# Layer-1 MLP: the second product with tokens on the partitions, seven eighths of it by Strassen's seven block products

## Chip, core and metric

The kernel runs on one core of a Trainium2 chip. The metric is the device time of one execution in microseconds (us). The engines are TensorE (PE; PEld is its weight load), VectorE (DVE), ScalarE (ACT), GpSimd (POOL) and SyncE (SP, which issues most of the DMAs).

## What is computed

The program is a two-layer trunk over 512 latent and 256 context tokens of width 1024. Layer 0 mixes by an mLSTM, layer 1 by windowed attention, and each layer ends in a squared-ReLU MLP of inner width 4096. The change touches only the MLP of layer 1, on the 512 latent tokens, and what follows it:

```
h   = h + gate_msa * attention(...)
u   = rms_norm(h, norm_ffn) * (1 + scale) + shift      # 512 x 1024
hid = square(relu(u @ w1))                             # 512 x 4096
h   = h + gate * (hid @ w2)                            # 512 x 1024
out = rms_norm(h, final_norm)                          # 512 x 1024
```

## The kernel before, in words

Every fp32 product runs in three passes: each operand is split into a rounded part and a rest (`split`, L927 on ACT makes the high part, L928 on DVE the low part), and `mm3` (L96 to L98) multiplies high by high, high by low and low by high into one PSUM bank. Weights come in units of 128x1024 (512 KB): `unit` starts a DMA from SP into one of three `raw` buffers and splits it into one of four pairs `whi`, `wlo` (`nraw` and `nsplit` in `open_ring`).

In layer 1 the hidden stream lies transposed: features on the partitions, 512 tokens along the free axis, in eight tiles `hL`. `ffn` loops over four chunks of 1024 hidden features. In a chunk, the first `dense` makes eight tiles of `hid` from eight units of `w1`, 24 matmuls of 512 columns each; `evac1` does relu on ACT (L901), the square on POOL (L902), and the split into `hH`, `hL_` on ACT and DVE (L904, L905). The second `dense` multiplies the chunk by eight units of `w2`, 24 matmuls each, and `evac2` adds each result, times its gate, to `hL` on DVE (L912). The first three units of the first chunk and the last two of the last are done in two halves of 256 tokens, A and B, so that the norm ahead (`norm_group`) and the norm behind overlap with matmuls. In the last chunk `norm_add` (L302, L306) sums squares, `norm_rc` (L319 to L324) and `norm_bc` (L332) make 1/rms by matmuls with ones, a power on POOL and a transpose back, and `final` (L1646, L1650) scales each `hL` tile and writes it out from the SP and ACT queues.

The order on each engine is fixed ahead of the run by a scheduler that works from the program's dependencies; an engine then takes its rows strictly in that order. Waits come from semaphores, and a tile's buffer is reused when its last reader is done.

## Time and profile before

| what | value |
|---|---|
| time, median of 3 runs | 1590.76 us (1590.04 to 1591.33) |
| the profiled execution: time, span | 1593.31 us, 1591.5 us |
| mean granted TensorE clock | 0.988 |
| busy share of the span: PE, PEld, DVE, ACT, POOL | 97%, 87%, 64%, 42%, 25% |

The span is cut in stretches to see which engine has idle time where; the chain that ended last and the groups of instructions say what one operation takes. PE's durations overlap (a matmul starts before the one ahead has ended), so the time of one matmul is read from the distance of two starts.

### The profile page before, as it was taken

The page shows a single profiled execution, that of the slowest core. Times are in us where ns is not written, and L with a number is a line of the kernel's source. Part 1 is how long each engine was busy: PE and PEld are TensorE (multiplying, and loading weights), DVE is VectorE, ACT ScalarE, POOL GpSimd, SP SyncE. Part 2 cuts the span into 40 slices and gives each one's busy share as a digit, 9 for nine tenths or more (in the row PEclk, how much of TensorE's full clock was granted, in tenths as well). Part 3 has the DMA queues.
Part 4 walks back from the last instruction along what each step waited for, and adds up shares of the span by engine and source line. Part 5 has one row for each costly group of instructions (what it writes and reads, how often), then busy time and mean ns, then how long its engine had stood idle before and what let it go on. Part 6 is the DMA issues. An engine that isn't in the chain of part 4 may idle for free.

```text
span 1591.5 us, 23868 instructions
## 1 busy us (share of the span) xinstructions
PE 1538.4 (97%) x9198; PEld 1378.8 (87%) x9198; DVE 1013.9 (64%) x1894; ACT 676.2 (42%) x1399; POOL 402.2 (25%) x378
## 2 busy tenths in 40 slices
PE   7989999999999999999999999989999999999997
PEld 5868888878889999999999998878878888888886
DVE  4665647488697879777667677777887533333333
ACT  4533333334573341432523545666675413232231
POOL 0221111113203222322332231344443302011122
PEclk9989999999999999999999999999999999999999
DMA  8422323234221434344344321010111233222321
GB/s 316 142 66 93 120 68 106 64 122 154 79 88 55 131 120 133 113 158 141 119 135 148 103 79 34 28 54 27 41 54 40 93 95 104 93 93 93 99 88 53
DMA packets 48856, 156.75 MB, mean 98 GB/s; under 512 B 5439, under 2 KB 11071, under 8 KB 48615
## 3 DMA queue, kind: packets, MB, share of 16 engines
q1 hardware_dynamic: 46992, 153.73, 29.6%
q8 instruction: 72, 1.18, 0.3%
q10 hardware_dynamic: 1751, 1.51, 0.3%
q14 instruction: 41, 0.34, 0.1%
HBM read 153.12 MB, written 2.10 MB: 98 GB/s over the span
## 4 chain that ended last, share of the span: by engine, by line
PE 71%; DVE 8%; issue 5%; POOL 5%; ACT 4%; DMA 1%; POOLq 0%; DVEq 0%; ACTq 0%
PE mm L97 17%; PE mm L96 17%; PE mm L98 17%; DVE adap L273 2%; PE p L98 2%; PE p L97 2%; PE p L96 2%; PE pt L1583 1%; PE pj L96 1%; PE pj L98 1%; PE pj L97 1%; DVE wlo L928 1%; PE at L844 1%; ACT whi L927 1%; PE av L1599 1%
## 5 line engine op out<-in xcount | busy, mean ns | idle before, releaser
L928 DVE TENSOR_TENSOR wlo<-raw,whi 128x1024 fp32r<-128x1024 f32 (+2 forms) x180 | 217.3, 1211 | 118.7 <-ACT whi L927 113.6
L927 ACT CAST whi<-raw 128x1024 fp32r<-128x1024 f32 (+2 forms) x183 | 183.4, 1007 | 250.6 <-PE mm L97 202.8
L96 PE MATMUL mm<-uH,whi 128*128 128x512 f32 (+1 forms) x488 | 189.1, 392 | 4.1 <-ACT v L710 3.9
L97 PE MATMUL mm<-uL,whi 128*128 128x512 f32 (+1 forms) x488 | 186.9, 386 | 0.1
L98 PE MATMUL mm<-uH,wlo 128*128 128x512 f32 (+1 forms) x488 | 186.4, 384 | 0.0
L273 DVE SCALAR_TENSOR_TENSOR adap<-raw,crow 128x1024 bf16<-128x1024 f32 x128 | 166.8, 1303 | 20.7 <-DMA raw<-ada 19.9
L96 PE MATMUL mm<-h,whi 128*128 128x384 f32 x512 | 174.1, 340 | 4.0 <-DVE hL L1161 2.2
L97 PE MATMUL mm<-h,whi 128*128 128x384 f32 x512 | 173.1, 338 | 0.5 <-DVE h L928 0.3
L98 PE MATMUL mm<-h,wlo 128*128 128x384 f32 x512 | 172.8, 337 | 0.0
L902 POOL TENSOR_TENSOR r<-r 128x512 f32<-128x512 f32 (+1 forms) x35 | 52.1, 1492 | 259.9 <-ACT r L901 259.9
L96 PEld LDWEIGHTS mm<-uH,whi 128*128 128x128 f32 x488 | 92.2, 191 | 20.8 <-ACT v L710 4.2
L98 PEld LDWEIGHTS mm<-uH,wlo 128*128 128x128 f32 x488 | 92.5, 190 | 18.0 <-issue 0.3
L97 PEld LDWEIGHTS mm<-uL,whi 128*128 128x128 f32 x488 | 92.7, 191 | 17.3 <-issue 1.0
L96 PE MATMUL mm<-hH,whi 128*128 128x512 f32 (+1 forms) x272 | 104.0, 382 | 0.0
L97 PE MATMUL mm<-hL,whi 128*128 128x512 f32 (+1 forms) x272 | 103.9, 382 | 0.0
L98 PE MATMUL mm<-hH,wlo 128*128 128x512 f32 (+1 forms) x272 | 103.9, 382 | 0.0
L927 ACT CAST whi<-sum 128x512 fp32r<-128x512 f32 (+1 forms) x42 | 31.9, 761 | 164.9 <-PE mm L97 84.2
L96 PEld LDWEIGHTS mm<-h,whi 128*128 128x128 f32 x512 | 96.8, 189 | 5.1 <-ACT h L927 2.6
L97 PEld LDWEIGHTS mm<-h,whi 128*128 128x128 f32 x512 | 96.8, 189 | 1.3 <-DVE h L928 1.2
L98 PEld LDWEIGHTS mm<-h,wlo 128*128 128x128 f32 x512 | 96.6, 189 | 0.0
L912 DVE SCALAR_TENSOR_TENSOR hL<-mm,mod,hL 128x512 f32<-128x512 f32 (+1 forms) x34 | 24.5, 720 | 102.8 <-PE mm L98 102.8
L98 PE MATMUL p<-t,wlo 128*128 128x384 f32 x224 | 75.5, 337 | 0.1
(355 smaller groups left out, 3966.4 us busy)
## 6 DMA issues: line engine op xcount, KB each, us to landing
raw<-w SPq DMA_DIRECT2D x96, 512.0 KB, 3.5
raw<-ada SPq DMA_DIRECT2D x80, 512.0 KB, 3.6
raw<-w2a SPq DMA_DIRECT2D x32, 512.0 KB, 3.5
adaw<-ada SPq DMA_DIRECT2D x16, 512.0 KB, 7.0
hL<-xT SPq DMA_DIRECT2D x16, 256.0 KB, 3.5
raw<-wqk SPq DMA_DIRECT2D x8, 512.0 KB, 3.9
raw<-wv SPq DMA_DIRECT2D x8, 512.0 KB, 3.6
raw<-wo SPq DMA_DIRECT2D x8, 512.0 KB, 3.5
```

The lines of the kernel that those rows point to most:

```text
L96: mm(out=out, lhsT=ah, rhs=bh, start=start, stop=False)
L97: mm(out=out, lhsT=ah, rhs=bl, start=False, stop=False)
L98: mm(out=out, lhsT=al, rhs=bh, start=False, stop=stop)
L273: self.tc.keep_in_program_order(nc.vector.scalar_tensor_tensor(out=pr, in0=w, scalar=0.5, in1=self.crow[:, v, :], op0=ALU.mult, op1=ALU.mu ...
L844: mm(out=o[hh][:, i * VW:(i + 1) * VW], lhsT=pw[g, d, hh][:, i, :], rhs=v[:, 3 * g + i, hh, :], start=False, stop=i == 2)
L902: nc.gpsimd.tensor_tensor(out=r, in0=r, in1=r, op=ALU.mult)
L912: nc.vector.scalar_tensor_tensor(out=h, in0=ps, scalar=self.mod[layer][:, 40 + m, v:v + 1], in1=h, op0=ALU.mult, op1=ALU.add)
L927: keep(self.nc.scalar.copy(out=hi, in_=src))
L928: keep((eng or self.nc.vector).tensor_tensor(out=lo, in0=src, in1=hi.bitcast(F32), op=ALU.subtract))
L1583: nc.tensor.transpose(out=pt[:, i * P:(i + 1) * P], in_=ps_[i][:, n * P:(n + 1) * P], identity=self.ident)
L1599: mm(out=o, lhsT=vv, rhs=pl, start=False, stop=n == len(blks) - 1)
```

## The change

**What it does.** `ffn` is replaced by `plan1` and `ffn1`. The product with `w1` stays as it was. The product with `w2` puts 128 tokens on the partitions (the hidden tile is the stationary operand, 512 columns of `w2` the moving one). The hidden features are taken in steps of 8, 8, 8 and 4 tiles of 128 (28 of 32). In a step the hidden part is a 2x2 matrix of blocks (256 tokens by half the features), `w2` a 2x2 matrix too (half the features by 512 outputs), and seven block products take the place of eight (the form with fifteen sums). A product is two PSUM tiles (two token tiles) of `nk` times 3 matmuls each. DVE makes the sums of the hidden blocks (`s12`, `s34` in `first` and `second`) and the differences of the `w2` blocks (`less`), in place in buffers `wb11` to `wb22`. Products 2 and 7 stay in PSUM over all steps; the other five are copied to, and from the second step on added to, SBUF tiles `acc`. `join` puts the blocks together, multiplies by the gate (`grow`, a row on all partitions) and adds them to `res`, which `turn` makes from `hL` by 32 transposes on PE. The last four hidden tiles are multiplied plainly, with `w2` times the gate as the moving operand. The final norm then runs by tokens: sum of squares along the free axis on ACT, a power on POOL, scaling on DVE and ACT, eight writes of 256 KB. The square of the hidden values moves from POOL to ACT. The first four hidden units instead of three run in halves. PSUM is cut into 4 + 4 banks instead of 5 + 3.

The core of the diff:

```diff
+        def less(o, x, y, u):
+
+            def f():
+                nc.vector.tensor_tensor(out=w2r[o, u], in0=w2r[x, u], in1=w2r[y, u], op=ALU.subtract)
+            return f
...
+        def w2(b, u, *extra):
+            def f():
+                hi, lo = [self.ring.tile([P, D], F32R, name=n, tag=n, bufs=self.nsplit) for n in ("whi", "wlo")]
+                self.split(w2r[b, u], hi, lo)
+                for x in extra:
+                    x()
+                return hi, lo
+            return f
...
+        for base, nk in self.steps1:
...
+            for b in (12, 22, 11, 21):
+                extra += [load(b, u, at + (11, 12, 21, 22).index(b) * len(us) + u) for u in us]
+            extra += [less(12, 12, 11, u) for u in us]
...
+            self.plan += [w1(m, *extra[per * i:per * i + per]) for i, m in enumerate(ms[skip:])]
+            self.plan += [w2(b, u) for b in (11, 21) for u in us]
+            self.plan += [w2(22, u, less(22, 22, 12, u)) for u in us]
+            self.plan += [w2(12, u, less(11, 22, 11, u)) for u in us]
+            self.plan += [w2(22, u, less(21, 22, 21, u)) for u in us]
+            self.plan += [w2(b, u) for b in (11, 21) for u in us]
...
+                raw = self.ring.tile([P, D], F32, name="raw", tag="raw", bufs=self.nraw)
+                nc.sync.dma_start(out=raw, in_=a["w2l"][i])
+                nc.vector.tensor_tensor(out=raw, in0=raw, in1=self.grow, op=ALU.mult)
+                hi, lo = [self.ring.tile([P, D], F32R, name=n, tag=n, bufs=self.nsplit) for n in ("whi", "wlo")]
+                self.split(raw, hi, lo)
+                return hi, lo
...
+            ws = [self.begun.pop(0) for _ in m]
...
+                for n, k in [(n, k) for k in range(4) for n in range(len(at))] + [(n, k) for n in range(len(at))
+                                                                                 for k in range(4, KT)]:
...
+                    self.mm3(pss[n], hi[:, sl], lo[:, sl], *xs[g](k), k == 0, k == KT - 1)
+                    if k == KT - 1:
+                        evac(m[at[n]], g, pss[n])
+                        if g in "BL":
+                            self.feed()
+
...
+        def first(m, k):
+
+            r = rt[m]
+            hid["11", k] = [self.base.tile([P, H], F32R, name="h11", tag=f"hC{2 * k + i}") for i in range(2)]
+            self.split(r[:, 0:H], *hid["11", k])
+            s = rt["34", k] = fp.tile([P, NL], F32, name="s34", tag="s34", bufs=2)
+            tt(out=s[:, 0:H], in0=r[:, 0:H], in1=r[:, H:NL], op=ALU.subtract)
+
+        def second(m, m0, k):
+
+            r0, r1, s34 = rt.pop(m0), rt.pop(m), rt.pop(("34", k))
+            hid["12", k] = two("h12", k)
+            self.split(r1, *hid["12", k])
+            s = fp.tile([P, NL], F32, name="s12", tag="s12", bufs=2)
+            tt(out=s[:, 0:H], in0=r0[:, H:NL], in1=r1[:, H:NL], op=ALU.add)
+            tt(out=s[:, H:NL], in0=s[:, 0:H], in1=r0[:, 0:H], op=ALU.subtract)
+            tt(out=s34[:, H:NL], in0=r1[:, 0:H], in1=s[:, H:NL], op=ALU.subtract)
+            for n, src in (("1", s), ("3", s34)):
+                hid[n, k] = two("e" + n, k)
+                self.split(src, *hid[n, k])
...
+            keep = p in (2, 7)
+            ws = [self.begun.pop(0) for _ in range(nk // 2)]
...
+            for i in range(2):
...
+                for k in range(nk):
...
+                    hi, lo = ws[k // 2]
+                    self.mm3(ps, *part(n, k, i), hi[:, sl], lo[:, sl], k == 0 and (c == 0 or not keep),
+                             k == nk - 1 and (end or not keep))
+                if keep:
+                    continue
+                if c == 0:
...
+                    nc.scalar.copy(out=acc[p, i], in_=ps)
+                else:
+                    tt(out=acc[p, i], in0=ps, in1=acc[p, i], op=ALU.add)
+            for _ in ws:
+                self.feed()
...
+        for c, (base, nk) in enumerate(self.steps1):
+            for k in range(nk):
...
+                    hidden([0, nk, 1, nk + 1], square, (("A", (0, 1)), ("A", (2, 3)), ("B", range(4))))
...
+            for p, n in ((1, "11"), (2, "12"), (3, "S4"), (5, "S1"), (6, "S2"), (7, "S3"), (4, "22")):
+                if c == len(self.steps1) - 1 and p == 6:
+                    self.rows1()
+                product(p, n, nk, c)
...
+        def turn(t):
+
+            res[t] = fp.tile([P, D], F32, name="res", tag=("w111", "w120", "w211", "w220")[t])
+            for d in range(2):
+                ps = self.mm.tile([P, 512], F32, name="mm", tag="mm")
+                for k in range(4):
+                    nc.tensor.transpose(out=ps[:, k * P:(k + 1) * P], in_=self.hL[4 * d + k][:, t * P:(t + 1) * P],
+                                        identity=self.ident)
+                nc.scalar.copy(out=res[t][:, d * 512:(d + 1) * 512], in_=ps)
...
+        def join(i):
+            a1, a3, a4, a5, a6 = [acc[p, i] for p in (1, 3, 4, 5, 6)]
+            x = fp.tile([P, NL], F32, name="r", tag="r", bufs=4)
+            for o, l, r, op in ((a6, a1, a6, ALU.add), (a1, kept[2, i], a1, ALU.add), (x, kept[7, i], a6, ALU.add),
+                                (a6, a6, a5, ALU.add), (a3, a3, a6, ALU.add), (a4, x, a4, ALU.subtract),
+                                (a5, x, a5, ALU.add)):
+                tt(out=o, in0=l, in1=r, op=op)
+            for t, d, o in ((i, 0, a1), (i, 1, a3), (2 + i, 0, a4), (2 + i, 1, a5)):
+                tt(out=o, in0=o, in1=self.grow[:, d * 512:(d + 1) * 512], op=ALU.mult)
+                y = res[t][:, d * 512:(d + 1) * 512]
+                tt(out=y, in0=y, in1=o, op=ALU.add)
...
+        for n, m in enumerate(range(self.last1, 4 * KT)):
+            hidden([m], square)
+            hp.append(two("h12", n))
+            self.split(rt.pop(m), *hp[n])
+            turn((0, 2, 1, 3)[n])
+            if n % 2:
+                join(n // 2)
...
+        for t in (0, 2, 1, 3):
...
+                for k, (hh, hl) in enumerate(hp):
+                    self.mm3(ps, hh[:, t * P:(t + 1) * P], hl[:, t * P:(t + 1) * P], ws[k][0][:, ds], ws[k][1][:, ds],
+                             k == 0, k == len(hp) - 1)
+                y = res[t][:, ds]
+                tt(out=y, in0=ps, in1=y, op=ALU.add)
+                nc.scalar.activation(out=junk[d], in_=y, func=AF.Square, accum_out=sv[:, d:d + 1])
+                o = os[d] = fp.tile([P, NL], F32, name="r", tag="r", bufs=4)
+                tt(out=o, in0=y, in1=self.frow[:, ds], op=ALU.mult)
+            tt(out=sv[:, 2:3], in0=sv[:, 0:1], in1=sv[:, 1:2], op=ALU.add)
+            nc.vector.tensor_scalar(out=sv[:, 2:3], in0=sv[:, 2:3], scalar1=1.0 / D, scalar2=EPS, op0=ALU.mult,
+                                    op1=ALU.add)
+            nc.gpsimd.tensor_tensor(out=sv[:, 2:3], in0=sv[:, 2:3], in1=self.mhalf[:, 0:1], op=ALU.pow)
+            nc.vector.tensor_scalar(out=os[0], in0=os[0], scalar1=sv[:, 2:3], scalar2=None, op0=ALU.mult)
+            nc.scalar.activation(out=os[1], in_=os[1], func=AF.Copy, scale=sv[:, 2:3])
+            nc.sync.dma_start(out=out[t, :, 0:512], in_=os[0])
+            nc.scalar.dma_start(out=out[t, :, 512:D], in_=os[1])
...
+        nc.sync.dma_start(out=self.frow, in_=self.a["fin"].broadcast_to([P, D]))
...
-        self.mm = self.ctx_mm2.enter_context(tc.tile_pool(name="mm2", bufs=5, space=PSUM, reuse_waits="tile"))
-        self.at = self.ctx_mm2.enter_context(tc.tile_pool(name="at2", bufs=3, space=PSUM, reuse_waits="tile"))
-        self.ctx_np = self.open_np()
+        self.mm = self.ctx_mm2.enter_context(tc.tile_pool(name="mm2", bufs=4, space=PSUM, reuse_waits="tile"))
+        self.at = self.ctx_mm2.enter_context(tc.tile_pool(name="at2", bufs=4, space=PSUM, reuse_waits="tile"))
+        ctx_np = self.open_np()
+        self.plan1()
...
+                self.feed()
+                self.feed()
...
-        def final(g):
-            bc = self.norm_rstd(self.st, g)
-            for k in range(KT):
-                o = self.hview(g, k)
-                nc.vector.scalar_tensor_tensor(out=o, in0=o, scalar=self.nrm[:, 4, k:k + 1], in1=bc,
-                                               op0=ALU.mult, op1=ALU.mult)
-                eng = nc.sync if k % 2 else nc.scalar
-                c0 = 0 if g == "A" else 256
-                eng.dma_start(out=out[k, :, c0:c0 + 256], in_=o)
-        self.ffn(1, self.u1, "L", "A", "B", final)
+        self.ffn1(self.u1, out)
+        self.ctx_ff1.close()
...
-    o["w2"] = np.stack([_mblocks(w[1][c * D:(c + 1) * D]) for c in range(NFC)])
+    t = w[1].reshape(4 * KT, P, 2, 512)
+    us = []
+    for base, nk in ((0, 4), (8, 4), (16, 4), (24, 2)):
+        for fh in range(2):
+            for d in range(2):
+                us += [t[base + nk * fh + 2 * i:base + nk * fh + 2 * i + 2, :, d].transpose(1, 0, 2).reshape(P, D)
+                       for i in range(nk // 2)]
+    o["w2b"] = np.ascontiguousarray(np.stack(us))
+    o["w2l"] = np.ascontiguousarray(w[1][28 * P:]).reshape(4, P, D)
+    o["fin"] = f["final_norm"].reshape(1, D)
```

**How the order on the engines moves.** Up to the last eight tiles of the attention's output product the order on all engines is the same in both kernels. VectorE while `w2` is multiplied, before (the first tiles of a chunk; `wlo` is the low part of the unit for a later tile, `hL` the sum of the tile just finished):

```order
L912 SCALAR_TENSOR_TENSOR hL0_3350<-mm_14023,mod1_82,hL0_3350 128x512
L928 TENSOR_TENSOR wlo_14148<-raw_14145,whi_14147 128x1024
L912 SCALAR_TENSOR_TENSOR hL1_3361<-mm_14055,mod1_82,hL1_3361 128x512
L928 TENSOR_TENSOR wlo_14180<-raw_14177,whi_14179 128x1024
L912 SCALAR_TENSOR_TENSOR hL2_3372<-mm_14087,mod1_82,hL2_3372 128x512
L928 TENSOR_TENSOR wlo_14212<-raw_14209,whi_14211 128x1024
L912 SCALAR_TENSOR_TENSOR hL3_3383<-mm_14119,mod1_82,hL3_3383 128x512
```

and now, in the third step while products 3 and 5 run (`wb` are blocks of `w2`, `acc` the sums of products 3; a row whose first name has `mm` behind the arrow reads PSUM):

```order
L877 TENSOR_TENSOR wlo_14829<-wb22_14406,whi_14828 128x1024
L877 TENSOR_TENSOR wlo_14834<-wb22_14408,whi_14833 128x1024
L1175 TENSOR_TENSOR wb22_14406<-wb22_14406,wb12_14396 128x1024
L1175 TENSOR_TENSOR wb22_14408<-wb22_14408,wb12_14398 128x1024
L877 TENSOR_TENSOR wlo_14863<-wb12_14396,whi_14862 128x1024
L1175 TENSOR_TENSOR wb11_14444<-wb22_14406,wb11_14444 128x1024
L877 TENSOR_TENSOR wlo_14868<-wb12_14398,whi_14867 128x1024
L1175 TENSOR_TENSOR wb11_14446<-wb22_14408,wb11_14446 128x1024
L1319 TENSOR_TENSOR acc_13643<-mm_14872,acc_13643 128x512
L1175 TENSOR_TENSOR wb21_14454<-wb22_14406,wb21_14454 128x1024
L1319 TENSOR_TENSOR acc_13658<-mm_14886,acc_13658 128x512
```

Between two tiles there was one unit to split and one sum; now a product of the same length has two units to split, up to two differences of 128x1024 and two sums.

TensorE at the end of the program, before (the last matmuls of half B, then the norm's products with ones and its transposes):

```order
L98 MATMUL mm_15489<-hH_6_14845,wlo_15401 128x256
L96 MATMUL mm_15489<-hH_7_14847,whi_15400 128x256
L97 MATMUL mm_15489<-hL_7_14848,whi_15400 128x256
L98 MATMUL mm_15489<-hH_7_14847,wlo_15401 128x256
L319 MATMUL at_15517<-ones_63,ssB_15171 128x1
L319 MATMUL at_15517<-ones_63,sq_15515 128x1
L319 MATMUL at_15517<-ones_63,ssB_15171 128x1
L319 MATMUL at_15517<-ones_63,sq_15515 128x1
L332 MATMUL at_15526<-ident_61,rc_15524 128x128 x2
```

and now, between the second and third plain hidden tile:

```order
L97 MATMUL mm_15442<-uL7_12888,whi_15347 128x512
L98 MATMUL mm_15442<-uH7_12887,wlo_15348 128x512
L1349 MATMUL mm_15481<-ident_61,hL0_3350 128x128
L1349 MATMUL mm_15481<-ident_61,hL1_3361 128x128
L1349 MATMUL mm_15481<-ident_61,hL2_3372 128x128
L1349 MATMUL mm_15481<-ident_61,hL3_3383 128x128
L1349 MATMUL mm_15487<-ident_61,hL4_3523 128x128
L1349 MATMUL mm_15487<-ident_61,hL5_3534 128x128
L1349 MATMUL mm_15487<-ident_61,hL6_4116 128x128
L1349 MATMUL mm_15487<-ident_61,hL7_4127 128x128
L96 MATMUL mm_15509<-uH0_12873,whi_15365 128x512
```

The products with ones at the end are gone; eight transposes of `hL` stand behind each of the last four hidden tiles, in front of the next one.

VectorE near the end, before (the last unit, the last whole sums, half A of the last two tiles, the start of the norm):

```order
L928 TENSOR_TENSOR wlo_15401<-raw_15398,whi_15400 128x1024
L912 SCALAR_TENSOR_TENSOR hL4_3523<-mm_15293,mod1_82,hL4_3523 128x512
L912 SCALAR_TENSOR_TENSOR hL5_3534<-mm_15331,mod1_82,hL5_3534 128x512
L912 SCALAR_TENSOR_TENSOR hL6_4116<-mm_15369,mod1_82,hL6_4116 128x256
L912 SCALAR_TENSOR_TENSOR hL7_4127<-mm_15404,mod1_82,hL7_4127 128x256
L322 TENSOR_SCALAR rs_15437<-at_15432 128x2
```

and now, during the last four hidden tiles (`raw` times `grow` is the gate put into `w2`, `h12` the low part of a hidden tile, the rest `join`):

```order
L1219 TENSOR_TENSOR raw_15419<-raw_15419,grow_15314 128x1024
L877 TENSOR_TENSOR wlo_15388<-raw_15385,whi_15387 128x1024
L1219 TENSOR_TENSOR raw_15470<-raw_15470,grow_15314 128x1024
L1359 TENSOR_TENSOR acc_13582<-kept_13607,acc_13582 128x512
L1361 TENSOR_TENSOR acc_13582<-acc_13582,grow_15314 128x512
L877 TENSOR_TENSOR wlo_15423<-raw_15419,whi_15422 128x1024
L1363 TENSOR_TENSOR res_15429<-res_15429,acc_13567 128x512
L1219 TENSOR_TENSOR raw_15537<-raw_15537,grow_15314 128x1024
L877 TENSOR_TENSOR h12_15426<-r_15416,h12_15426 128x512
L1219 TENSOR_TENSOR raw_15588<-raw_15588,grow_15314 128x1024
L1359 TENSOR_TENSOR r_15493<-kept_13746,acc_13721 128x512
L877 TENSOR_TENSOR wlo_15474<-raw_15470,whi_15473 128x1024
```

The rows of `join` stand between the splits that the next matmuls need.

## Rows read from the trace of the kernel before

**Rows 1.** Busy time by stretches of the span, whole layer-1 MLP; columns named in the first row.
```profile
core 0: us, PE busy (x) PEld busy (x) DVE busy (x) ACT busy (x) POOL busy (x), PEclk, DMA share, GB/s
...
1300.00:1400.00 100.00, 100.00 (x435) 81.50 (x434) 35.31 (x37) 27.85 (x34) 12.70 (x8) 1.00 0.29 95
...
1560.00:1592.00 32.00, 23.18 (x154) 20.60 (x152) 10.11 (x24) 3.12 (x8) 6.59 (x10) 0.88 0.19 66
```

**Rows 2.** Timeline, TensorE, last whole matmuls: start, duration, engine, line, operation, tiles, shape.
```profile
1555.19 0.39 PE L96 MATMUL mm<-hH,whi 128*128 128x512 f32 x1
...
1568.26 0.39 PE L98 MATMUL mm<-hH,wlo 128*128 128x512 f32 x1
1568.49 0.29 PE L96 MATMUL mm<-hH,whi 128*128 128x256 f32 x1
1568.61 0.28 PE L97 MATMUL mm<-hL,whi 128*128 128x256 f32 x1
```

**Rows 3.** Timeline, TensorE, four transposes of the attention and the follower.
```profile
1204.95 0.60 PE L1583 MATMUL pt<-ident,e 128*128 128x128 f32 x4
1205.30 0.36 PE L96 MATMUL mm<-y,whi 128*128 128x256 f32 x1
```

**Rows 4.** Groups by shape, TensorE, from 990 us on; count, busy, mean ns, idle before.
```profile
L1583 PE MATMUL pt<-ident,e 128*128 128x128 f32 x288 | 45.1, 277 | 2.2 <-POOL e L1567 2.1
```

**Rows 5.** Groups by shape, VectorE, layer-1 MLP.
```profile
L928 DVE TENSOR_TENSOR wlo<-raw,whi 128x1024 fp32r<-128x1024 f32 x62 | 76.0, 1226 | 65.7 <-ACT whi L927 61.0 <-PE mm L98 1.9
L912 DVE SCALAR_TENSOR_TENSOR hL<-mm,mod,hL 128x512 f32<-128x512 f32 x30 | 22.5, 751 | 97.8 <-PE mm L98 97.8
L905 DVE TENSOR_TENSOR hL<-r,hH 128x512 fp32r<-128x512 f32 x29 | 20.1, 693 | 45.9 <-ACT hH L904 45.9
...
L905 DVE TENSOR_TENSOR hL<-r,hH 128x256 fp32r<-128x256 f32 x6 | 2.9, 489 | 1.3 <-ACT hH L904 1.1
```

**Rows 6.** Timeline, VectorE, one low part of a weight unit and its follower.
```profile
1226.06 1.22 DVE L928 TENSOR_TENSOR wlo<-raw,whi 128x1024 fp32r<-128x1024 f32 x1
1227.19 0.48 DVE L343 SCALAR_TENSOR_TENSOR uL<-nt,mod,uH 128x256 fp32r<-128x256 f32 x1
```

**Rows 7.** Groups by shape, ScalarE, layer-1 MLP.
```profile
L927 ACT CAST whi<-raw 128x1024 fp32r<-128x1024 f32 x61 | 64.2, 1052 | 166.5 <-PE mm L97 162.4 <-issue 3.9
L904 ACT CAST hH<-r 128x512 fp32r<-128x512 f32 x29 | 18.0, 620 | 49.2 <-POOL r L902 49.2
L901 ACT ACTIVATE r<-mm 128x512 f32<-128x512 f32 x29 | 17.1, 591 | 0.0
```

**Rows 8.** Stretches around the one long TensorE wait ahead of the MLP (columns as rows 1).
```profile
1211.20:1213.40 2.20, 0.25 (x4) 0.04 (x2) 1.14 (x4) 1.13 (x5) 1.94 (x3) 1.00 0.00 0
1215.00:1219.00 4.00, 4.00 (x24) 4.00 (x23) 1.95 (x5) 1.89 (x4) 2.07 (x3) 0.57 0.00 0
```

**Rows 9.** Timeline, TensorE, the two waits in the first matmuls of the MLP.
```profile
1224.50 0.61 PE L319 MATMUL at<-ones,ssB 128*128 128x1 f32 x4 [0.79 <-DVE ssB L306]
...
1226.15 0.43 PE L332 MATMUL at<-ident,rc 128*128 128x128 f32 x2 [0.35 <-POOL rc L324]
```

**Rows 10.** Timeline, TensorE, the last matmul.
```profile
1581.62 0.28 PE L98 MATMUL mm<-hH,wlo 128*128 128x256 f32 x1
```

**Rows 11.** Timeline, end of the program, VectorE and POOL.
```profile
1583.86 0.16 DVE L322 TENSOR_SCALAR rs<-at 128x2 f32<-128x2 f32 x1 [1.44 <-PE at L319]
1585.58 3.22 DVE L1646 SCALAR_TENSOR_TENSOR hL<-hL,sm,at 128x256 f32<-128x256 f32 x8 [1.57 <-PE at L332]
...
1584.10 0.71 POOL L324 TENSOR_TENSOR rc<-rs,mhalf 128x2 f32<-128x2 f32 x1 [1.38 <-DVE rs L322]
```

**Rows 12.** DMA issues: count, KB each, median us from issue to landing.
```profile
raw<-w SPq DMA_DIRECT2D x96, 512.0 KB, 3.5
...
outT<-hL SPq DMA_DIRECT2D x8, 128.0 KB, 1.7
```

**Rows 13.** Waits in the layer-1 MLP: engine, line, on what; total us, times, longest.
```profile
ACT whi L927 <- PE mm L97: 162.4, 55, 4.6
```

More of the change, by code (lines that the diff above doesn't have):

```diff
@@ L127, in dense_steps @@
             yield
-    @staticmethod
-    def order(n, head, tail, first, second, mid):
-        out = [(m, first) for m in range(head)] + [(m, second) for m in range(head)]
-        for m in range(head, n - tail):
-            out += [(m, g) for g in mid]
-        out += [(m, first) for m in range(n - tail, n)] + [(m, second) for m in range(n - tail, n)]
-        return out
     def setup(self):
@@ new lines, in rows1 @@
+    def rows1(self):
+        nc = self.nc
+        self.grow = self.fp.tile([P, D], F32, name="grow", tag="w121")
+        self.frow = self.fp.tile([P, D], F32, name="frow", tag="w221")
+        nc.sync.dma_start(out=self.frow, in_=self.a["fin"].broadcast_to([P, D]))
+        for d in range(2):
+            ps = self.mm.tile([P, 512], F32, name="mm", tag="mm")
+            for k in range(4):
+                nc.tensor.transpose(out=ps[:, k * P:(k + 1) * P],
+                                    in_=self.mod[1][:, 40 + 4 * d + k, 0:1].broadcast_to([P, P]), identity=self.ident)
+            nc.scalar.copy(out=self.grow[:, d * 512:(d + 1) * 512], in_=ps)
@@ L1392, in layer1_mix @@
                 bc["A"] = self.norm_bc(rc)
+                self.feed()
+                self.feed()
         for c in "AB":
@@ L1395, in layer1_mix @@
         self.u1 = u
+        ctx_np.close()
+        self.ctx_ff1 = ExitStack()
+        self.fp = self.ctx_ff1.enter_context(tc.tile_pool(name="ff1", bufs=1, reuse_waits="tile"))
     def split_y(self, g, ys=None):
@@ L1708, in pack @@
     w = f["ffn_w2"]
-    o["w2"] = np.stack([_mblocks(w[1][c * D:(c + 1) * D]) for c in range(NFC)])
+    t = w[1].reshape(4 * KT, P, 2, 512)
+    us = []
+    for base, nk in ((0, 4), (8, 4), (16, 4), (24, 2)):
+        for fh in range(2):
+            for d in range(2):
+                us += [t[base + nk * fh + 2 * i:base + nk * fh + 2 * i + 2, :, d].transpose(1, 0, 2).reshape(P, D)
[3 more added lines that the diff above has]
+    o["fin"] = f["final_norm"].reshape(1, D)
     o["w2a"] = np.ascontiguousarray(np.stack([_mblocks(w[0][c * 512:(c + 1) * 512]) for c in range(2 * NFC)])
@@ L1757 @@
            for n, a in arrays.items()}
-    out = nc.dram_tensor("outT", (KT, P, NL), F32, kind="ExternalOutput").ap()
+    out = nc.dram_tensor("out", (NL // P, P, D), F32, kind="ExternalOutput").ap()
     with tile.TileContext(nc) as tc:
@@ L1761 @@
     r = run_bass_kernel_spmd(nc, [arrays], core_ids=[0])
-    o = np.asarray(r.results[0]["outT"]).reshape(D, NL)
-    return np.ascontiguousarray(o.T).reshape(1, NL, D)
+    return np.asarray(r.results[0]["out"]).reshape(1, NL, D)
```

128 lines of the change are left out of this document (89 added, 39 removed).

## Prediction

> **What bounds the kernel now.** I read the busy time by stretches first, to see which engine is full where the change works. Through the layer-1 MLP TensorE is busy 100 of 100 us at full granted clock, while VectorE has 35.31, ScalarE 27.85, POOL 12.70 and the DMA engines a share of 0.29 [rows 1]; only in the last 32 us does TensorE fall to 23.18. So this stage is as long as its matmuls, and a matmul taken out shortens the program, as long as nothing else becomes late. The price of a matmul is the distance of two starts on the timeline, not its duration, since they overlap: 57 matmuls of 512 columns go from 1555.19 to 1568.49, 0.2333 us each, though each is shown with 0.39; one of 256 columns takes 0.12 [rows 2]. That is the higher of the clock's two levels, 2.4 GHz.
>
> **The sum.** All terms are against the profiled execution: span 1591.5 us, its own time 1593.31, which is 2.55 above the median of 1590.76. I carry the difference over to the median.
>
> *Matmuls.* Before, the product with `w2` was 4 chunks x 8 units x 24 = 768 matmuls of 512 columns. Now it is 28/32 of 768 = 672, times 7/8 = 588, and 4/32 of 768 = 96 plain ones: 684. The `w1` product has the same columns (four units in halves instead of three). 84 fewer x 0.2333 = **-19.6 us**.
>
> *Transposes.* 32 for `res` and 8 for `grow`, in ten groups of four, on TensorE's own queue. A group like them, four fp32 transposes of 128x128, held TensorE for 0.35 us until its follower started [rows 3]: **+3.5 us**. One by one they would take 277 ns each [rows 4], 40 x 0.277 = 11.1 us; that is the upper bound. I take the lower one, since the row of four is the same operation in the same form between the same matmuls. The Trainium skill (TensorE: Matmul & The Clock Gate, Part 4: PE-mode transpose) gives a transpose about 275 ns in one kernel's context; the duration here agrees, but read as a cost it would make the sum 7.6 us longer, and the distances of this trace speak against that reading.
>
> *The norm on TensorE.* From 1568.49 to 1581.62 lie 95 matmuls of 256 columns, 95 x 0.12 = 11.4 us; it takes 13.1 us [rows 2, 10]. The 1.7 us between are the norm's products with ones, its transposes and half A's waits, and they go: **-1.7 us**.
>
> *The tail.* Before, 9.9 us lie between the start of the last matmul and the end of the span [rows 10]. Now follow one matmul (0.39 [rows 2]), one sum out of PSUM (0.75, as L912 in [rows 5]), a square (0.59, as L901 in [rows 7]), two column-sized VectorE rows (0.16 each), the power on POOL (0.71 [rows 11]), a scaling (0.59), six hand-overs of an estimated 0.1, and the write. Before, the write ended 2.7 us after the last VectorE row (1585.58 + 3.22 = 1588.80), with 1.7 us from issue to landing of 128 KB; a load of 512 KB takes 3.5 [rows 11, 12]. For 256 KB I take 3.2 in place of the 2.7, and 2.7 to 4.5 as bounds. Sum 7.15: **-2.7 us** (-3.2 to -1.4).
>
> *Waits for VectorE in a full step.* A step of eight tiles is 192 + 168 = 360 matmuls, 84.0 us of TensorE. VectorE has 22 units to split and 8 differences, 30 x 1.226 = 36.8; for each of four pairs of hidden tiles three rows of 512 and five of 256, 4 x (3 x 0.693 + 5 x 0.489) = 18.1; ten sums, 10 x 0.751 = 7.5 [rows 5]. That is 62.4 of 84.0, and in the seven products alone 20 x 1.226 + 7.5 = 32.0 of 39.2. Three products in a row have two splits, two differences and two sums, 6.4 us against 5.6 of TensorE: 2.4 us late in all. The four pairs of `whi`, `wlo` hold one product ahead, 5.6 us, so this costs nothing; without that lead it would cost 2.4 in each step. ScalarE's 22 casts (23.1 us) and its two passes over the hidden values stay under 50 us. POOL is out of it. The DMAs bring the same bytes; a `w2` buffer is free only after its last reader, but a load lands in 3.5 us [rows 12] and has most of a step. I cost all this at zero.
>
> *Waits at the end.* In the last, half-size step a product is only 2.8 us, and one split, one difference and two sums are 3.95: three such products lose 3.5 us against a lead of 2.8. Then, from the first sum of that step to the last split of the plain hidden tiles, VectorE has 15 rows of 1024 (18.4), ten sums (7.5), 29 rows of 512 (20.1, among them `join`) and two of 256: 47.0 us by durations. TensorE needs in that time 19.6 + 0.7 - 1.4 for products and `grow` and 4 x (5.6 + 0.7) for hidden tiles and `res`: 44.1. By distances a row is 0.09 shorter (1226.06 to 1227.19 against 1.22 [rows 6]), 5 us over 56 rows, and VectorE ends just in time. Last, the fourth hidden tile must be squared and split (0.59 + 0.59 + 0.62 + 0.69 [rows 5, 7]), and TensorE has only nine matmuls, 2.1 us, to fill that. I take 0.5 for the products and 1.0 here: **+1.5 us**, with 0 and 8 as bounds, the upper one if the rows run at full duration and both lags add.
>
> *The start.* The two waits there, 0.79 and 0.35 us [rows 9], are for the norm, which stays. Four units in half A give 11.3 us of work before half B is wanted, where there were 8.5. Zero.
>
> Sum: -19.6 + 3.5 - 1.7 - 2.7 + 1.5 = **-19.0 us**. Span 1572.5, this execution 1574.3, median **1572 us**. Its own range is 1567 (no waits, fastest write, the start's waits gone) to 1576.
>
> **Rivals.**
>
> *VectorE bounds the end.* It takes its rows in order, and `join` stands between the splits that the next matmuls need. For: the 47.0 against 44.1 above. Against: the same by distances, and TensorE may run four PSUM tiles ahead of VectorE's sums. With the 8 us of the bound it would be 1572 + 6.5 = 1578.5. Chance 0.20.
>
> *Transposes one at a time,* if each group drains TensorE first: 11.1 for 3.5, 1579.5. Chance 0.04. The figure of the Trainium skill (TensorE: Matmul & The Clock Gate, Part 4) read as a cost gives 40 x 0.275 = 11.0 us and the same time, an estimate.
>
> *Slower: the clock falls at the product boundaries.* Place: the first matmul of each block product, whose two units must be split, while ScalarE can write them only when the matmuls of the product before the last have freed the slots; it already waits 162.4 us for that in this stage [rows 13]. Price: ahead of the MLP TensorE waited 1.95 of the 2.2 us from 1211.20, and then, from 1215 to 1219, had a granted clock of 0.57, that is mostly the lower level, 1.2 GHz [rows 8]: 1.95 + 4 x 0.43 = 3.7 us for each such wait. There are 27 boundaries; from six on the gain is gone, and with ten the time is 1609. For: the splits a product needs rise from one unit to two. Against: 32.0 of 39.2 us, a margin of about 1 us a product. Chance 0.05.
>
> *Less than it says:* the block products run at a longer distance, now that the hidden tile is the stationary operand and the weights stream. At 0.265 instead of 0.2333 for 588 matmuls the 19 us are gone: 1591. For: no matmul of this stage has its operands that way round, so no row of it prices that. Against: nothing in the rows ties the distance to anything but the columns. Chance 0.05.
>
> **How the numbers follow.** The forecast, 1567 to 1576, has 0.66. The range takes in the first two rivals, up to 1581, and leaves out the last two: 1567 to 1581. A change within 0.2% (3.2 us, about what a measurement of this kernel can tell from none) comes only from the last rival: 0.03 of its 0.05, the rest split. Faster 0.91, same 0.03, slower 0.06.
>
> **What would show it.** TensorE should have 84 matmuls fewer of 512 columns' worth from 1221 us on and still 0.233 us between starts inside a product; its idle time before block products should sum to under 2 us. VectorE should rise to about three quarters of the stage, with POOL near zero. The ten groups of transposes should take about 0.35 us each. After the last matmul about 7 us should follow. I am wrong if TensorE waits for `wlo` at many products, if its clock falls below 1.00 inside the MLP, or if the wait before the plain products is longer than 3 us; the time would then lie above 1581.

## The result and the profile after

The changed kernel takes **1568.43 us** median (1565.95 to 1573.33, 4 runs), the kernel before 1590.42 (1590.04 to 1591.33): a ratio of **0.9865**, 95% interval 0.984 to 0.9889. The prediction was 1572 us, 1567 to 1581. The profiled execution has a span of 1571.5 us and its own time of 1573.33; it is the longest of the four. Its stages against the span of before:

| | before | after | difference |
|---|---|---|---|
| first matmul of the layer-1 MLP at | 1221.66 | 1226.29 | +4.63 |
| from there to the start of the last matmul | 359.96 | 338.03 | -21.93 |
| from there to the end of the span | 9.88 | 7.18 | -2.70 |
| span | 1591.5 | 1571.5 | -20.0 |

The first line is no part of the change: up to the last eight tiles of the attention's output product every engine has the same order in both kernels, and the run of the changed kernel again (below) begins its MLP at 1221.32. The other two lines give **-24.6 us**, where the prediction had -19.0. So the time came out near the forecast with two deviations in it that nearly cancel, and that part of the agreement is luck; the experiments separate them.

Busy time by stretches, kernel after (columns as rows 1):

```profile
core 0: us, PE busy (x) PEld busy (x) DVE busy (x) ACT busy (x) POOL busy (x), PEclk, DMA share, GB/s
1300.00:1400.00 100.00, 100.00 (x443) 82.81 (x442) 65.94 (x80) 50.03 (x65) 0.00 (x0) 1.00 0.37 121
1400.00:1500.00 100.00, 100.00 (x443) 82.81 (x442) 68.83 (x90) 52.36 (x73) 0.00 (x0) 1.00 0.21 69
1540.00:1560.00 20.00, 19.97 (x92) 16.32 (x91) 18.61 (x34) 8.41 (x18) 1.10 (x2) 1.00 0.10 39
1560.00:1571.00 11.00, 4.71 (x21) 3.57 (x19) 4.97 (x12) 3.62 (x8) 1.08 (x2) 0.83 0.32 122
```

TensorE is still full at full clock. VectorE has gone from 35.31 [rows 1] to 66 and 69 of 100 us (the prediction said three quarters), ScalarE from 27.85 to 50 and 52, POOL to nothing. TensorE now begins 443 matmuls in 100 us where it began 435: they follow one another more closely. The timeline of TensorE, kernel after, at the end of a product and the start of the next hidden tile, and at the last matmuls, shows by how much:

```profile
1311.32 0.39 PE L96 MATMUL mm<-whi,h 128*128 128x512 f32 x1
1311.55 0.39 PE L97 MATMUL mm<-wlo,h 128*128 128x512 f32 x1
1311.78 0.39 PE L98 MATMUL mm<-whi,h 128*128 128x512 f32 x1
1312.00 0.39 PE L96 MATMUL mm<-uH,whi 128*128 128x512 f32 x1
...
1554.80 0.39 PE L98 MATMUL mm<-whi,h 128*128 128x512 f32 x1
...
1564.32 0.39 PE L98 MATMUL mm<-whi,h 128*128 128x512 f32 x1
```

42 matmuls from 1554.80 to 1564.32 are 0.2267 us each, not the 0.2333 of [rows 2]. The kernel before had both distances. Its timeline in a hidden tile, which the prediction did not look at:

```profile
1324.93 0.39 PE L96 MATMUL mm<-uH,whi 128*128 128x512 f32 x1
...
1327.65 0.39 PE L96 MATMUL mm<-uH,whi 128*128 128x512 f32 x1
```

Twelve matmuls in 2.72 us, 0.2267 each: the product with `w1` had the short distance, the product with `w2` the long one. A full step's products, from their first matmul to the next hidden tile, are now 38.08 us = 168 x 0.2267, three times alike; before it was 44.79 = 192 x 0.2333. No product waits.

The transposes, timeline of TensorE, kernel after (`turn`, two groups of four shown as one row):

```profile
1522.58 1.04 PE L1349 MATMUL mm<-ident,hL 128*128 128x128 f32 x8
1523.38 0.48 PE L96 MATMUL mm<-uH,whi 128*128 128x512 f32 x1
```

Eight transposes hold TensorE for 0.80 us, 0.10 each. Groups by shape, VectorE, kernel after (counts and durations of the rows that the prediction multiplied):

```profile
L877 DVE TENSOR_TENSOR wlo<-wb,whi 128x1024 fp32r<-128x1024 f32 x49 | 59.2, 1222 | 35.9 <-ACT whi L876 35.8
L1175 DVE TENSOR_TENSOR wb<-wb,wb 128x1024 f32<-128x1024 f32 x28 | 33.6, 1220 | 1.9 <-DMA wb<-w2b 1.9
L1319 DVE TENSOR_TENSOR acc<-mm,acc 128x512 f32<-128x512 f32 x30 | 20.3, 686 | 1.0 <-PE mm L98 0.8
```

VectorE waits 35.8 us for the casts ahead of its low parts, and only 0.8 for TensorE's sums. The end, timeline of all engines, kernel after:

```profile
1564.32 0.39 PE L98 MATMUL mm<-whi,h 128*128 128x512 f32 x1
1564.75 0.69 DVE L1385 TENSOR_TENSOR res<-mm,res 128x512 f32<-128x512 f32 x1 [1.14 <-PE mm L98]
1565.47 0.63 ACT L1386 ACTIVATE junk<-res 128x512 f32<-128x512 f32 x1 [1.82 <-DVE res L1385]
...
1566.66 0.54 POOL L1392 TENSOR_TENSOR ss<-ss,mhalf 128x1 f32<-128x1 f32 x1 [4.90 <-DVE ss L1390]
1567.23 0.72 ACT L1394 ACTIVATE r<-r,ss 128x512 f32<-128x512 f32 x1 [1.04 <-POOL ss L1392]
...
1567.99 0.34 ACTq L1396 DMA_DIRECT2D out<-r  x1
```

It is the chain that the prediction summed. The write issued at 1567.99 lands 2.7 us later, and the span ends some 0.9 us behind that, at 1571.5; of the prediction's 3.2 us for the write a part was thus this end of the span, which the kernel before has too.

### The profile page after: what moved, and what is told of

Read it like the earlier page. It is cut to its first block, busy times and chain, and to the rows that moved or that the text cites. A ratio compares the mean times of both kernels' runs of the same rounds, so it can differ in the third digit from the quotient of the medians.

```text
span 1571.5 us, 23851 instructions
## 1 busy us (share of the span) xinstructions
PE 1519.8 (97%) x9110; PEld 1365.5 (87%) x9110; DVE 1123.5 (71%) x2064; ACT 744.2 (47%) x1506; POOL 341.3 (22%) x333
## 4 chain that ended last, share of the span: by engine, by line
PE 71%; DVE 8%; issue 6%; POOL 5%; ACT 4%; DMA 1%; POOLq 0%; DVEq 0%; ACTq 0%
PE mm L96 16%; PE mm L97 16%; PE mm L98 16%; DVE adap L261 2%; PE p L98 2%; PE p L96 2%; PE p L97 2%; PE pt L1793 1%; PE pj L96 1%; PE pj L98 1%; PE pj L97 1%; DVE wlo L877 1%; PE at L832 1%; ACT whi L876 1%; PE av L1809 1%
## 5 line engine op out<-in xcount | busy, mean ns | idle before, releaser
L877 DVE TENSOR_TENSOR wlo<-raw,whi 128x1024 fp32r<-128x1024 f32 (+2 forms) x152 | 182.6, 1205 | 87.9 <-ACT whi L876 87.1
L876 ACT CAST whi<-raw 128x1024 fp32r<-128x1024 f32 (+2 forms) x155 | 154.0, 1000 | 139.1 <-PE mm L97 74.7
L96 PE MATMUL mm<-uH,whi 128*128 128x512 f32 (+1 forms) x496 | 191.4, 390 | 3.9 <-ACT v L698 3.9
L97 PE MATMUL mm<-uL,whi 128*128 128x512 f32 (+1 forms) x496 | 188.8, 382 | 0.4 <-DVE uL L331 0.4
L98 PE MATMUL mm<-uH,wlo 128*128 128x512 f32 (+1 forms) x496 | 188.9, 382 | 0.0
L96 PE MATMUL mm<-h,whi 128*128 128x384 f32 x512 | 173.7, 339 | 4.0 <-DVE hL L1110 2.2
L97 PE MATMUL mm<-h,whi 128*128 128x384 f32 x512 | 172.9, 338 | 0.5 <-DVE h L877 0.5
L98 PE MATMUL mm<-h,wlo 128*128 128x384 f32 x512 | 172.6, 337 | 0.0
L96 PEld LDWEIGHTS mm<-uH,whi 128*128 128x128 f32 x496 | 94.0, 191 | 19.8 <-ACT v L698 4.2
L98 PEld LDWEIGHTS mm<-uH,wlo 128*128 128x128 f32 x496 | 94.5, 191 | 17.9 <-issue 0.3
L97 PEld LDWEIGHTS mm<-uL,whi 128*128 128x128 f32 x496 | 94.6, 191 | 17.0 <-issue 1.0
L96 PEld LDWEIGHTS mm<-h,whi 128*128 128x128 f32 x512 | 96.4, 188 | 5.2 <-ACT h L876 2.6
L97 PEld LDWEIGHTS mm<-h,whi 128*128 128x128 f32 x512 | 96.4, 188 | 1.3 <-DVE h L877 1.2
L98 PEld LDWEIGHTS mm<-h,wlo 128*128 128x128 f32 x512 | 96.5, 188 | 0.0
L877 DVE TENSOR_TENSOR wlo<-wb,whi 128x1024 fp32r<-128x1024 f32 x49 | 59.2, 1222 | 35.9 <-ACT whi L876 35.8
L877 DVE TENSOR_TENSOR h<-r,h 128x384 fp32r<-128x384 f32 (+2 forms) x100 | 56.6, 568 | 35.4 <-ACT h L876 35.2
L876 ACT CAST whi<-wb 128x1024 fp32r<-128x1024 f32 x49 | 51.6, 1054 | 60.9 <-PE mm L97 27.1
L98 PE MATMUL p<-t,wlo 128*128 128x384 f32 x224 | 75.4, 337 | 0.3 <-DVE wlo L877 0.3
L97 PE MATMUL p<-t,whi 128*128 128x384 f32 x224 | 75.2, 336 | 0.0
L96 PE MATMUL p<-t,whi 128*128 128x384 f32 x224 | 75.2, 336 | 0.0
```

Of the source, the lines that this page charges most:

```text
L96: mm(out=out, lhsT=ah, rhs=bh, start=start, stop=False)
L97: mm(out=out, lhsT=ah, rhs=bl, start=False, stop=False)
L98: mm(out=out, lhsT=al, rhs=bh, start=False, stop=stop)
L876: keep(self.nc.scalar.copy(out=hi, in_=src))
L877: keep((eng or self.nc.vector).tensor_tensor(out=lo, in0=src, in1=hi.bitcast(F32), op=ALU.subtract))
```

## The experiments

Each run's stages are read as in the table above; "the MLP" is the time from its first matmul to the start of its last. The kernel after had 338.03 us there and 7.18 behind.

**The changed kernel again** (no edit).

> The changed kernel once more, unaltered. In its first profile the layer-1 MLP starts 4.6 us later than before (1226.29 against 1221.66 us), although every engine's order is the same up to there, and its four times lie 7.4 us apart (1565.95 to 1573.33) where those of the kernel before lie 1.3 apart. Theory: the lost time is of that one execution, in the part ahead of the MLP; then a new profile has its first MLP matmul at another time (1219 to 1226), while from the first MLP matmul to the last one it again takes 338.0 us (within 0.5) and 7.2 us from there to the end. Rival: the change itself moves the earlier part; then the first MLP matmul is at 1226 again.

Median 1571.64 us against 1593.35 of the kernel before in the same session, ratio 0.9864 (0.9846 to 0.9882). Timeline of TensorE, first and last matmul of its MLP:

```profile
1221.32 0.52 PE L96 MATMUL mm<-uH,whi 128*128 128x256 f32 x3
...
1558.91 0.39 PE L98 MATMUL mm<-whi,h 128*128 128x512 f32 x1
```

The start is at 1221.32 (before: 1221.66), the MLP 337.59 us, the rest 7.19, the span 1566.1. So the 4.63 us were of that one execution. In the profiles of this study that share the code ahead of the MLP it starts between 1218.74 and 1226.29. Where this arises is seen only in part. In the late execution the first 40 us moved 306 GB/s instead of 315, and from 260 to 440 us the clock was 0.97 instead of 0.98; that these are the cause is not shown (the run `two_pairs` below moved 306 GB/s there too, and its MLP began 2.8 us earlier). And the one long wait ahead of the MLP [rows 8], 1.95 us in each of the three profiles, was followed by different clocks. Stretches of TensorE at and behind that wait, kernel after (the columns are us, busy time, granted clock, DMA):

```profile
1217.26:1219.46 2.20, 0.25 (x3) 1.00 0.00 0
1219.46:1221.26 1.80, 1.80 (x14) 1.00 0.00 0
1221.26:1223.26 2.00, 2.00 (x18) 1.00 0.00 0
```

The same of the changed kernel again:

```profile
1209.56:1211.76 2.20, 0.25 (x4) 1.00 0.00 0
1211.76:1213.56 1.80, 1.80 (x9) 0.58 0.00 0
1213.56:1215.56 2.00, 2.00 (x11) 0.50 0.00 0
1215.56:1218.56 3.00, 3.00 (x16) 0.50 0.00 0
```

From the end of the wait to the first MLP matmul it takes 6.83 us at full clock, 9.56 with the clock at the lower level, and took 8.27 in the kernel before: 2.7 us of spread from one wait. All eleven profiles of this study have this wait, 1.95 us long. In seven no fall of the clock followed (6.8 us to the MLP), in three a short one (8.2 to 8.4 us), in one the long one. The larger part of the spread is older: the wait itself ended between 1210.86 and 1219.46 us.

**Eight block products in the same layout (`eight`).** The differences of `less`, the combinations in `first` and `second`, and `kept` go, and each hidden tile is split once. `product` becomes this loop (shortened; the operands of `mm3` partly in words):

```
for fh in range(2):
    ws = [self.begun.pop(0) for _ in range(nk // 2)]
    for t in range(4):
        for k in range(nk): self.mm3(pss[t], h[fh, k] of token tile t, ws ...)
```

> The same layout, joins and end, but the product with w2 as eight plain block products, 96 matmuls in place of 84 for each half of a step: 84 more matmuls of 512 columns, no differences of weights, hidden combinations or kept sums, so VectorE and ScalarE have much less to do. Theory (the stage is as long as its matmuls): 84 x 0.2267 = 19.0 us longer than the changed kernel from the first MLP matmul to the last, 357 in place of 338, with the distance still 0.2267 us. What then stands against the kernel before (359.96) is the layout alone: about -3 there and -2.7 behind the last matmul. Rival (VectorE or ScalarE eat part of what the seven products save): fewer than 15 us longer. Rival (the seven products save nothing, the gain is the layout's): 0 to 3 us longer.

Median 1587.29 us, ratio to before 0.9961 (0.9947 to 0.9974). The MLP is 356.85 us, 18.8 more than after and 19.3 more than after run again; the rest 7.02. A full step's products take 43.52 us = 192 x 0.2267. Busy time by stretches (columns as rows 1):

```profile
1300.00:1400.00 100.00, 100.00 (x443) 82.84 (x442) 31.56 (x32) 35.20 (x46) 0.00 (x0) 1.00 0.28 95
```

So the seven products give all that their count gives (the first theory), although VectorE does twice the work for them, 65.94 of 100 us against 31.56, and ScalarE 50.03 against 35.20; that work lies beside the matmuls. Against the kernel before, the layout by tokens, with all else that the change brings, is worth 3.1 us in the MLP and 2.9 behind it.

**The residual's transposes twice.** `for k in (0, 1, 2, 3, 0, 1, 2, 3)` in `turn`.

> Each of the 32 transposes of the residual is done twice into the same place (the second time over the first). Theory (they overlap like other matmuls, 0.1 us each): 32 x 0.1 = 3.2 us more in the MLP, and no wait behind them. Rival (each costs its whole duration): 32 x 0.272 = 8.7 us more. Rival (TensorE has slack there because VectorE sets the end): 0 to 1 us more.

Median 1574.36 us, ratio to before 0.9869 (0.985 to 0.9888). The MLP is 341.20 us, 3.2 to 3.6 more than in the two profiles of the changed kernel. Timeline of TensorE, 16 transposes and the follower:

```profile
1515.01 1.91 PE L1349 MATMUL mm<-ident,hL 128*128 128x128 f32 x16
1516.68 0.48 PE L96 MATMUL mm<-uH,whi 128*128 128x512 f32 x1
```

1.67 us for 16 where eight took 0.80: 0.10 each while the row's own mean is 272 ns. The Trainium skill (TensorE: Matmul & The Clock Gate, Part 4: PE-mode transpose) gives a transpose about 275 ns in one kernel's context; the duration of 272 ns agrees, but as a price in a row of transposes it is nearly three times too high here.

**The kernel before with its hidden high parts elsewhere in SBUF.**

```diff
-hid["L"] = [(fp.tile([P, NL], F32R, name=f"hH_{k}", tag=f"hH_{k}"),
+hid["L"] = [(self.base.tile([P, NL], F32R, name=f"hH_{k}", tag=f"uC{k}"),
```

> The kernel before, with the eight high parts of the hidden tiles in other tiles of SBUF: at 4 to 20 KB of a partition in place of 126 to 158 KB; the low parts stay there. In the kernel before, matmuls that stream a hidden tile followed one another after 0.2333 us, those that stream the normed input (20 to 52 KB) after 0.2267. Theory (the place of the streamed tile makes the difference): the matmuls with the high parts, two of three in the product with w2, go to 0.2267, those with the low parts stay nearer 0.2333: 480 x 0.0066 = 3.2 us less in the MLP, half of that if one slow matmul in three still spoils its neighbours. Rival (it lies in the product itself, its sums on VectorE or its shape): all stay at 0.2333 and the time is the same within 0.3 us.

Median 1588.18 us, ratio to before 0.9968 (0.9958 to 0.9979); the MLP is 356.66 us, 3.3 less. Timeline of TensorE in a product with `w2`:

```profile
1360.18 0.39 PE L96 MATMUL mm<-hH,whi 128*128 128x512 f32 x1
1360.40 0.40 PE L97 MATMUL mm<-hL,whi 128*128 128x512 f32 x1
1360.64 0.39 PE L98 MATMUL mm<-hH,wlo 128*128 128x512 f32 x1
1360.86 0.39 PE L96 MATMUL mm<-hH,whi 128*128 128x512 f32 x1
```

Over the 720 matmuls those that stream a moved tile have 0.2267 us (L96) and 0.2258 us (L98) to the next start, those that stream a low part, which stays in its pool, 0.2342 (L97); in the kernel before all three had 0.2333. The edit changes addresses and nothing else, so addresses can change the distance of the same instructions on the same values: the first theory.

**The low parts moved instead.** The same edit on `hL_`.

> The counterpart of the run with the high parts moved: the kernel before, with the eight low parts of the hidden tiles at 4 to 20 KB and the high parts at 127 to 143 KB. Theory (the place of the tile that is streamed sets the distance, whichever tile it is): the 240 matmuls that stream a low part go from 0.2333 to 0.2267 us, the 480 with the high parts stay at 0.2333: 240 x 0.0066 = 1.6 us less than 359.96 from the first MLP matmul to the last. Rival (it was something about the high parts): all stay at 0.2333. Rival (where the one lies beside the other counts, not where it lies): both change, as it would have been seen with the high parts if the low ones had followed.

One execution took 1590.39 us beside 1590.86 of the kernel before; a single pair of times can't tell them apart. The MLP is 356.91 us, 3.05 less, twice what was expected. The matmuls with a low part came to 0.2259 us, those with a high part to 0.2304 on average, nearly half of the way, although the high parts had stayed in their pool. In a triple one matmul is slow, the one with a high part against `whi` (0.2324); with `wlo` the high part streams faster (0.2284). So the addresses matter, but not by a line between low and high for the streamed tile alone: the stationary tile may count too, or where one tile lies beside the other, as the last rival had it. The theory in this form is refuted, and the mechanism stays open.

**Two of four slots held back in the products (`two_pairs`).**

```diff
+            if nk == 4 and p == 1:
+                for _ in ws:
+                    held.append([self.ring.tile([P, D], F32R, name=n, tag=n, bufs=self.nsplit) for n in ("whi", "wlo")])
...
+            if nk == 4 and p == 4:
+                for t in [t for x in held for t in x]:
+                    tt(out=idle[:, 0:1], in0=t[:, 0:1].bitcast(F32), in1=acc[p, 1][:, 0:1], op=ALU.add)
+                held.clear()
...
+            for _ in range(n if nk == 2 else {1: 0, 4: 2 * n}.get(p, n)):
```

> In each full step two of the four pairs of slots for the split weights are held back from the third product to the last (their contents are not used), so that a product's units can be split only when the product before has let its own slots go. This makes the waits at the product boundaries that the slower rival spoke of: five in a full step, 15 in all. A unit's slot is free after 18 of 24 matmuls (4.1 us of 5.4), its cast takes 1.05 and its low part 1.2, and a difference of weights may stand between: TensorE waits an estimated 1 to 3 us at each. Theory (a wait costs itself, the clock stays): the MLP 15 to 45 us longer than 338 us, the granted clock 1.00 in it. The rival's price (each such wait is followed by some 4 us at 0.57, 1.7 us more): 40 to 70 us longer, and a granted clock visibly under 1.00 in the three stretches of products.

Behind product 1 of a full step two pairs are taken and not used; behind product 4, the last, they are read and let go. Median 1589.71 us, ratio to before 0.9969 (0.9955 to 0.9983); the MLP is 358.68 us, 20.7 more. TensorE's waits in it (us in all, times, longest), and two stretches of products (columns as rows 1):

```profile
PE mm L97 <- DVE wlo L877: 9.6, 11, 1.5
PE kept L97 <- DVE wlo L877: 1.6, 3, 0.5
PE mm L98 <- DVE wlo L877: 0.5, 1, 0.5
...
1365.00:1405.00 40.00, 34.83 (x144) 25.98 (x143) 28.24 (x28) 12.57 (x12) 0.00 (x0) 1.00 0.34 118
1450.00:1490.00 40.00, 35.53 (x148) 26.91 (x147) 27.23 (x30) 12.19 (x16) 0.00 (x0) 1.00 0.19 66
```

The waits come where the rival put them, 15 of up to 1.5 us, and the clock stays at 1.00 with TensorE idle for 5 of 40 us. As shown they sum to 11.7 us. The products of the three full steps took 18.7 us more. The 14 starts behind a wait in them account for 13.6 us of it (the view hides the first 0.16 us of a wait under a matmul that is shown with 0.39 where the next could start after 0.2267). The matmul after each took 0.34 us to the next start, 1.5 us in all, and 399 of the other 476 stood 0.229 us or more apart, 3.6 us in all, where none of the changed kernel's did. So the first theory holds for the clock, but a wait cost more than itself. Holding back two of the four pairs costs 20.7 us, and the rival's waits would have eaten the gain, though not through the clock.

**The low parts of the `w2` units twice (`w2lo2`).**

```diff
 self.split(w2r[b, u], hi, lo)
+nc.vector.tensor_tensor(out=lo, in0=w2r[b, u], in1=hi.bitcast(F32), op=ALU.subtract)
```

> Each low part of a w2 unit is computed twice, the second time over the first with the same values: 14 more VectorE rows of 128x1024 in a full step, 7 in the last. By the prediction's count a full step then has 62.4 + 14 x 1.22 = 79.5 us of VectorE for 84.0 of TensorE, and its seven products 32.0 + 17.1 = 49.1 for 39.2 (by distances, 0.09 less a row, 46); 7 to 10 us late, of which one product of lead hides 5.6. Theory (VectorE has about 1 us of margin in a product, as counted): 1 to 4 us of waiting in each of the second and third step, less in the first, where ScalarE copies the sums, and 2 to 6 in the last step: the MLP 4 to 14 us longer. Rival (VectorE is far from mattering): under 1 us longer. Rival (VectorE already bounds the products): 14 x 1.13 x 3 = 47 us longer.

Median 1585.51 us, ratio to before 0.994 (0.9925 to 0.9956); the MLP is 357.11 us, 19.1 to 19.5 more: between the theory and the second rival. A full step's products take 44.0 us in place of 38.08 in the second and third step, 40.7 in the first, and the last step's 4.2 more. Stretches (columns as rows 1), the first in the second step, the others in the last:

```profile
1365.00:1405.00 40.00, 35.67 (x151) 27.53 (x150) 37.98 (x39) 13.09 (x14) 0.00 (x0) 1.00 0.46 158
...
1517.00:1520.00 3.00, 1.34 (x8) 0.63 (x6) 3.00 (x4) 1.99 (x2) 0.00 (x0) 1.00 0.00 0
1520.00:1524.00 4.00, 3.57 (x11) 2.98 (x12) 4.00 (x6) 1.17 (x2) 0.00 (x0) 0.57 0.00 0
```

VectorE is now full, 37.98 of 40 us, and sets the pace. By distances its rows of one step's products are 28 low parts and 6 differences of 1.13 and 10 sums of 0.60, 44.4 us; the products took 44.0, so the lead hid 0.4 us and not 5.6. In the last step TensorE was idle for 1.66 of 3.0 us, and there the clock did fall, to 0.57 for some 4 us, 1.7 us of cost. Timeline of TensorE in this run, the longest wait in a full step with what follows it, and the wait ahead of the fall:

```profile
1386.07 0.50 PE L97 MATMUL kept<-wlo,e 128*128 128x512 f32 x1 [1.58 <-DVE wlo L1190]
1386.40 0.39 PE L98 MATMUL kept<-whi,e 128*128 128x512 f32 x1
...
1387.79 0.39 PE L98 MATMUL kept<-whi,e 128*128 128x512 f32 x1
...
1390.96 0.39 PE L98 MATMUL kept<-whi,e 128*128 128x512 f32 x1
...
1519.30 0.65 PE L1408 MATMUL mm<-ident,mod 128*128 128x128 f32 x4 [1.61 <-DVE acc L1320]
```

The wait of 1.58 us was followed by no fall, the one of 1.61 by one. And the long distance is back: six matmuls from 1386.40 to 1387.79 are 0.2317 us each, the 14 behind them 0.2264, though this edit adds no tile and moves none. So a matmul's distance does not hang on the addresses alone; behind a wait it is longer for a few matmuls, and why is open.

**More VectorE work at the end.** The same repetition for the plain units and the plain hidden tiles.

> The low parts of the four plain w2 units and of the four plain hidden tiles are computed twice, the second time over the first: 4 x 1.13 + 4 x 0.6 = 6.9 us more of VectorE between the last block product and the first plain one. Theory (VectorE has a margin there of a few us, since TensorE waits only 0.2 to 0.4 us before the plain products now): 1.5 to 5 us of waiting before the plain products. Rival (VectorE sets the end, as the rival of the prediction had it): 6.9 us more. Rival (wide margin): under 0.5 us.

Median 1570.24 us, ratio to before 0.9845 (0.9829 to 0.9861). TensorE's waits from 1500 us on:

```profile
PE mm L96 <- DVE res L1388: 1.5, 1, 1.5
PE mm L98 <- DVE h L1371: 0.4, 1, 0.4
```

The MLP is 340.03 us, 2.0 to 2.4 more for 6.9 us of work: a margin of some 4.7 us, as the theory had it. The wait moved to the sums out of PSUM (L1388 there is L1385 after).

**Less VectorE work at the end.** `nc.gpsimd.tensor_tensor` for the product with `grow` in `join`, the additions one hidden tile later.

> The eight multiplications of the kept sums by the gate go from VectorE to POOL, which has nothing to do there, and the eight additions behind them stand a hidden tile later: 8 x 0.69 = 5.5 us less for VectorE at the end. Theory (TensorE waits only 0.2 to 0.4 us there): the MLP at most 0.4 us shorter, no difference that the times can show. Rival (VectorE bounds the end): 2 us or more shorter.

Median 1569.15 us, ratio to before 0.9836 (0.9822 to 0.9851), which overlaps that of the changed kernel. The MLP is 338.80 us and the rest 7.66, nothing gained, so VectorE does not bound the end by these 5.5 us. No run gave a version that is shown to beat the changed kernel.

## Why the prediction was right, and where its steps were not

- **Matmuls, -19.6.** This term was mis-sized: the price was taken from the product with `w2` of before (0.2333) and used for matmuls that run at 0.2267 now. The count was right (`eight`: 84 more cost 18.8 to 19.3, at 0.2267). 768 x 0.2333 - 684 x 0.2267 = 179.2 - 155.1 = **-24.1**. The sentence that failed is that nothing in the rows ties the distance to anything but the columns: the `w1` matmuls of the same trace stood at 0.2267. The runs with moved tiles show that addresses can make this difference. That the addresses of the streamed weights are why the new products have the short distance would fit, but was not tried on the changed kernel, and the runs `two_pairs` and `w2lo2` have the long distance in its products too, in `w2lo2` behind waits and without any tile moved. What sets the distance stays open.
- **Transposes, +3.5.** The 40 took 3.98 us; the twofold run shows the same price at the margin. The matmul behind each row of eight took 0.32 us to the next start in place of 0.23, five times 0.09, which stands in the terms below.
- **The norm on TensorE, -1.7.** The last chunk of before was 46.72 us to its last matmul against 44.79 of the others: -1.9.
- **The tail, -2.7.** It took 7.18 us against 7.15 summed, which is -2.70.
- **Waits in a full step, 0.** There were none. The margin was smaller than its lead made it look: the repeated low parts made VectorE 6.3 us late by count, and 5.9 of it came through. The prediction's claim that the four pairs matter is borne out, though its price of 2.4 us a step without that lead was far too small: holding two back cost 4.2, 7.8 and 6.8 us in the three steps.
- **Waits at the end, +1.5.** They were some 0.5: VectorE had about 4.7 us in hand where the sum by durations had it late.
- **The start, 0.** All `w1` stretches together, without the transposes, came out 0.4 us shorter; three short waits are left at the start.
- Sum: -24.1 + 4.0 - 1.9 - 2.7 + 0.5 - 0.4 = **-24.6**, as measured; the execution's late start gave 4.6 back, and left -20.0.
- **Rivals.** VectorE at the end is refuted by the two runs that gave it more and less work there, transposes one at a time by the twofold run. The clock at product boundaries: neither the waits nor the fall came; where waits of up to 1.58 us were made in full steps, the clock stayed. Less than it says, by a longer distance: the reverse came.

The median moved by 22.0 us, between the 20.0 of this profile and the 25.4 of the changed kernel's second one (1566.1 against 1591.5), since each execution begins its MLP at its own time; that this accounts for the distance of the medians from -24.6 is argued, for only the profiled executions show their stages. With the right price and its other terms as they stood, the prediction's sum is -23.5 and its median 1567.3, at the low end of the range that it gave. That end is itself looser than its working: no waits (-1.5), the fastest write (-0.5) and the start's waits gone (-1.1) lead from 1571.8 to 1568.7, not to 1567, and the measured median of 1568.43 lies in the part for which no term was named.

## What to carry to other kernels

Price a matmul by the distance of starts in each stretch of the trace apart, and ask of two stretches with the same shape and different distances what differs, the addresses of the tiles too. Seven products for eight paid in full here because VectorE's added work stayed under TensorE's time over a step's products (28.6 of 38.1 us by count and distances) and the split weights had a whole product of slots as lead, which covered the three products in which it did not (5.7 of 5.4 us): check both by the product, not by the stage. Compare stages from their own first instruction, since equal code ahead of the change began its last stage up to 7.6 us apart.
